# Squares, key scaling and rotary products of layer 1's attention on GpSimd

## The chip, the core and the metric

One core of a Trainium2 chip runs the whole program. Its engines are TensorE (matmul, with its own weight loads), VectorE, ScalarE, GpSimd and SyncE, which issues the transfers. The metric is the device time of one execution in microseconds (us). The kernel before takes 1248.55 us, the median of three runs (1248.15 to 1248.75).

## What is computed

Two decoder layers over 512 tokens of width 1024. Layer 0 mixes tokens with a gated recurrence, layer 1 with multi-head latent attention; beside each mixer four heads attend to a memory of 256 rows, and each layer ends with an MLP that has a causal convolution. The change concerns layer 1's six heads:

```python
q = (rms_norm(cq, qa_g) @ w_uq).reshape(B, S, MLA_HEADS, MLA_QK)              # 128 + 64 columns a head
kv = (rms_norm(ckv, kva_g) @ w_ukv).reshape(B, S, MLA_HEADS, MLA_NOPE + MLA_VDIM)
k_nope, v = kv[..., :MLA_NOPE], kv[..., MLA_NOPE:]
k = jnp.concatenate([k_nope, k_rope], axis=-1)                                # k_rope is the same for all heads
q = rms_norm(q, qn_g)
k = rms_norm(k, kn_g)
q = jnp.concatenate([q[..., :MLA_NOPE], apply_rope(q[..., MLA_NOPE:], cos, sin)], axis=-1)
k = jnp.concatenate([k[..., :MLA_NOPE], apply_rope(k[..., MLA_NOPE:], cos, sin)], axis=-1)
o = causal_block_attention(q, k, v)
```

## The kernel before

All matrix products are made in float32 precision: an operand is split into a rounded high part and the rest (`split`: ScalarE writes the high part, VectorE subtracts), and three matmuls are summed in PSUM. Weights come in tiles of up to 128x1024 (`raw`), are split into `whi` and `wlo`, and stay in a ring of three raw and two split tiles. PSUM has four `acc` tiles for projections, two `at` tiles for scores and two `tp` tiles for transposes.

Layer 1's attention works on three groups g of two heads. The list ORDER names its steps: Q and K project a group's queries and keys (`project_q`, `project_kv`), R normalizes and rotates its queries (`rotary_q`), S scales its keys (`scale_k`), T and U transpose queries and keys of one head, A attends, and M is one half of the memory attention:

```python
ORDER = "Q0 M0 K1 K0 R0 M1 S0 U00 Q1 R1 T00 T01 U01 A00 T10 S1 U10 A01 T11 Q2 K2 U11 S2 A10 A11 R2 U20 U21 T20 T21 A20 A21"
```

This is the order in which the code asks for the steps; the tile scheduler that builds the program then moves instructions, so that steps overlap, and fixes one sequence for each engine at build time. On the chip every engine takes its instructions in that sequence and waits on semaphores where an operand or a buffer isn't ready.

A projection's result leaves PSUM through ScalarE (`ev_q`, `ev_kv`, one for each of four tiles of 128 tokens). There, ScalarE also squares the two heads' columns and sums them (`square_sum`, an activation whose accumulator is read by a second instruction). `rotary_q` and `scale_k` turn the sums into reciprocal roots (`rsqrt`, twelve small VectorE steps), multiply the 64 rotary columns of q by the gain, and rotate them (`rotate`, six VectorE operations of 256 elements). `scale_k` multiplies the keys by the root, one VectorE operation for each tile and head, and writes the scaled rotary key twice into `ks`, as a product and a copy. The scratch of the squares and of the rotation lies in the buffers of the residual's tiles (`head_tile`, xl in the trace). ScalarE then rounds the rotated q (tile `qr`), and VectorE subtracts.

Of the kernel before, what the change touches and what calls it, by code (L numbers as in the profile page):

```python
# [8 lines left out]
F32 = mybir.dt.float32  # L9
# [3 lines left out]
AF = mybir.ActivationFunctionType  # L13
ALU = mybir.AluOpType
AX = mybir.AxisListType

P = 128
# [79 lines left out]
def hybrid_trunk_kernel(ctx, tc, x, mem, params, pos, wts, out, tap):  # L97
# [80 lines left out]
    def tt(o, a, b, op):  # L178
        nc.vector.tensor_tensor(out=o, in0=a, in1=b, op=op)  # L179

# [562 lines left out]
    with ExitStack() as l1:  # L743
# [41 lines left out]
        def rotate(o, a, nh, w):  # L785

            shape = [P, NT, nh, HALF]
            c = cost.unsqueeze(2).broadcast_to(shape)
            s = sint.unsqueeze(2).broadcast_to(shape)
            x1, x2 = a[:, :, :, 0:HALF], a[:, :, :, HALF:]  # L790
            for dst, p, q, op in ((o[:, :, :, 0:HALF], c, s, ALU.subtract), (o[:, :, :, HALF:], s, c, ALU.add)):
                tt(dst, x1, p, ALU.mult)
                tt(w, x2, q, ALU.mult)
                tt(dst, dst, w, op)
# [57 lines left out]
        with tc.tile_pool(name="mla", bufs=1, reuse_waits="tile") as ap:  # L852
# [4 lines left out]
            def project_q(g):  # L857
# [3 lines left out]
                def ev_q(t, ps):  # L861
                    act(q[:, t], ps.rearrange("p (h c) -> p h c", c=QK), AF.Identity, scale=rcq[:, t:t + 1])
                    for h in range(2):
                        square_sum(q[:, t, h, :], QK, qss[:, t, h:h + 1])
# [4 lines left out]
            def square_sum(src, n, o):  # L869
                junk = head_tile(15, (P, QK), F32)  # L870
                act(junk[:, :n], src, AF.Square, accum_out=o)

            def project_kv(g):
# [4 lines left out]
                def ev_kv(t, ps):  # L878
                    act(kv[:, t], ps.rearrange("p (h c) -> p h c", c=2 * P), AF.Identity, scale=rck[:, t:t + 1])
                    for h in range(2):  # L880
                        square_sum(k[:, t, h, :], NOPE, kss[:, t, h:h + 1])
# [4 lines left out]
            def rotary_q(q, qss):  # L886
# [4 lines left out]
                tt(qrope, qrope, pcol("qn").unsqueeze(1).broadcast_to([P, 2 * NT, ROPE]), ALU.mult)  # L891
                rotate(ro, q[:, :, :, NOPE:], 2, head_tile(15, (P, NT, 2, HALF), F32))
# [5 lines left out]
            def scale_k(k, kss):  # L898
# [3 lines left out]
                for t in range(NT):  # L902
                    for h in range(2):
                        ts(k[:, t, h, :], k[:, t, h, :], rk[:, t, h:h + 1], None, ALU.mult)

                ks = ap.tile([P, NT * 2, 2, ROPE], F32, name="ks")
                tt(ks.rearrange("p (t h) a c -> p t h a c", h=2)[:, :, :, 0], kr.unsqueeze(2).broadcast_to([P, NT, 2, ROPE]),
                   rk.unsqueeze(3).broadcast_to([P, NT, 2, ROPE]), ALU.mult)
                nc.vector.tensor_copy(out=ks[:, :, 1], in_=ks[:, :, 0])
# [147 lines left out]
```

## Time and profile before

| what | us |
|---|---|
| median of three runs | 1248.55 |
| the profiled execution | 1248.88 |
| its span on the core | 1246.8 |
| TensorE busy, over the span | 1223.9 (98%) |
| VectorE busy, over the span | 755.1 (61%) |
| ScalarE busy, over the span | 558.5 (45%) |
| GpSimd busy, over the span | 18.7 (2%) |
| layer 1's attention, about | 720 to 850 |

The busy time of an engine is the time in which one of its instructions runs; what an engine waits for is a matter of the sequence, and is read from the waits and the timeline. GpSimd works only at the program's start, where it builds masks.

### The profile page before, as it was taken

Reading aid. Unit: us, or ns where it says so; the run is one execution under the profiler, and the core shown is the slowest. Engines: PE = TensorE matmul, PEld = TensorE weight load, DVE = VectorE, ACT = ScalarE, POOL = GpSimd, SP = SyncE. Lnnn points to the kernel's source line nnn. Section 1 sums busy time; section 2 is a strip of 40 time slices with the busy share of each in tenths; the row PEclk is TensorE's granted clock in tenths of the full one; section 3 lists DMA queues with packets and bytes.
Section 4 is the critical chain, followed back from the end, with each engine's and each line's share of the span. In section 5 each row is a group of like instructions: output and inputs, shape, how many; then the busy total and the mean of one; then the engine's idle time right before and its main releaser. Section 6 shows DMA issues by size and latency. Waiting matters only on the chain.

```text
span 1246.8 us, 15938 instructions
## 1 busy us (share of the span) xinstructions
PE 1223.9 (98%) x6106; PEld 1017.8 (82%) x6106; DVE 755.1 (61%) x1536; ACT 558.5 (45%) x966; POOL 18.7 (2%) x50
## 2 busy tenths in 40 slices
PE   6999999999999999999999999999999999999998
PEld 4869888888888888888889877777888888888887
DVE  6857575765776757652425758765665766764222
ACT  5463434433543434332325689754453444433211
POOL 6000000000000000000000000000000000000000
PEclk9999999999999999999999999999999999999999
DMA  6211222123232233323323312012223233322331
GB/s 238 80 52 60 77 68 69 53 84 91 96 101 101 85 102 101 97 90 101 102 85 111 119 33 77 33 34 68 85 85 102 87 102 99 102 94 92 116 120 51
DMA packets 31755, 110.44 MB, mean 89 GB/s; under 512 B 3776, under 2 KB 4160, under 8 KB 31680
## 3 DMA queue, kind: packets, MB, share of 16 engines
q1 hardware_dynamic: 31680, 109.43, 27.3%
q8 instruction: 48, 0.79, 0.3%
q14 instruction: 27, 0.22, 0.1%
HBM read 107.32 MB, written 2.10 MB: 88 GB/s over the span
## 4 chain that ended last, share of the span: by engine, by line
PE 92%; ACT 4%; DVE 3%; issue 1%; DMA 1%; SPq 0%; DVEq 0%; ACTq 0%
PE acc L171 63%; PE at L171 24%; PE tp L202 3%; PE tp L171 2%; ACT xl L191 1%; DVE wlo L179 1%; ACT whi L191 0%; ACT pr L191 0%; DMA mt<-in_mem 0%; ACT kv L191 0%; ACT yl L191 0%; ACT q L191 0%; ACT xh L191 0%; ACT yh L191 0%; PE at L202 0%
## 5 line engine op out<-in xcount | busy, mean ns | idle before, releaser
L179 DVE TENSOR_TENSOR wlo<-raw,whi 128x1024 fp32r<-128x1024 f32 (+2 forms) x201 | 240.0, 1195 | 374.5 <-ACT whi L191 367.3
L191 ACT ACTIVATE whi<-raw 128x1024 fp32r<-128x1024 f32 (+2 forms) x201 | 208.9, 1039 | 459.2 <-PE acc L171 298.8
L171 PE MATMUL acc<-xh,whi 128*128 128x512 f32 x616 | 241.1, 391 | 0.0
L171 PE MATMUL acc<-xh,wlo 128*128 128x512 f32 x616 | 240.8, 392 | 0.2 <-DVE wlo L179 0.2
L171 PE MATMUL acc<-xl,whi 128*128 128x512 f32 x616 | 240.9, 391 | 0.0
L171 PEld LDWEIGHTS acc<-xh,whi 128*128 128x128 f32 x616 | 115.7, 188 | 24.4 <-issue 1.0
L171 PEld LDWEIGHTS acc<-xh,wlo 128*128 128x128 f32 x616 | 115.5, 188 | 24.0 <-DVE wlo L179 0.4
L171 PEld LDWEIGHTS acc<-xl,whi 128*128 128x128 f32 x616 | 115.7, 188 | 23.6
L182 DVE SCALAR_TENSOR_TENSOR t<-u,par,t 128x510 f32<-128x510 f32 (+1 forms) x176 | 121.6, 746 | 4.2 <-ACT t L191 4.2
L171 PE MATMUL at<-xh,wlo 128*128 128x512 f32 x232 | 90.5, 390 | 0.0
L171 PE MATMUL at<-xl,whi 128*128 128x512 f32 x232 | 90.3, 389 | 0.0
L171 PE MATMUL at<-xh,whi 128*128 128x512 f32 x232 | 90.2, 389 | 0.0
L191 ACT ACTIVATE t<-u,par 128x512 f32<-128x512 f32 x88 | 67.0, 808 | 41.7 <-DVE u L179 41.7
L171 PE MATMUL acc<-wlo,xh 128*128 128x256 f32 (+2 forms) x224 | 67.1, 300 | 1.3 <-DVE wlo L179 1.3
L171 PE MATMUL acc<-whi,xh 128*128 128x256 f32 (+2 forms) x224 | 67.2, 302 | 0.5 <-ACT xh L191 0.4
L171 PE MATMUL acc<-whi,xl 128*128 128x256 f32 (+2 forms) x224 | 67.1, 301 | 0.0
L171 PE MATMUL acc<-whi,ah 128*128 128x512 f32 x132 | 51.3, 389 | 0.0
L171 PE MATMUL acc<-wlo,ah 128*128 128x512 f32 x132 | 51.3, 389 | 0.0
L171 PE MATMUL acc<-whi,al 128*128 128x512 f32 x132 | 51.3, 389 | 0.0
L171 PEld LDWEIGHTS at<-xl,whi 128*128 128x128 f32 x232 | 43.5, 188 | 9.1
L171 PEld LDWEIGHTS at<-xh,wlo 128*128 128x128 f32 x232 | 43.6, 188 | 9.0
L171 PEld LDWEIGHTS at<-xh,whi 128*128 128x128 f32 x232 | 43.5, 188 | 9.0
(333 smaller groups left out, 2143.4 us busy)
## 6 DMA issues: line engine op xcount, KB each, us to landing
raw<-in_w_up SPq DMA_DIRECT2D x88, 512.0 KB, 3.5
raw<-in_w_down SPq DMA_DIRECT2D x44, 512.0 KB, 3.5
raw<-in_hg_w_in SPq DMA_DIRECT2D x26, 512.0 KB, 3.6
raw<-in_w_out SPq DMA_DIRECT2D x16, 512.0 KB, 3.5
raw<-in_w_mem_kv SPq DMA_DIRECT2D x8, 512.0 KB, 4.6
mt<-in_mem SPq DMA_DIRECT2D x4, 512.0 KB, 4.7
xt<-in_x SPq DMA_DIRECT2D x4, 512.0 KB, 8.3
out<-u SPq DMA_DIRECT2D x8, 256.0 KB, 2.0
```

What stands on the lines that cost most here:

```text
L171: nc.tensor.matmul(ps, a, b, start=start, stop=stop)
L179: nc.vector.tensor_tensor(out=o, in0=a, in1=b, op=op)
L182: nc.vector.scalar_tensor_tensor(out=o, in0=a, scalar=s, in1=b, op0=op0, op1=op1)
L191: nc.scalar.activation(out=o, in_=a, func=f, **kw)
L202: nc.tensor.transpose(out=ps, in_=src, identity=ident)
```

## The change

The squares of q and k are made by GpSimd, for both heads of a tile in one product, into a new tile `sq2` with two buffers, and VectorE sums them (`square_sums`); ScalarE's squares are gone. The gain on q's rotary columns and the rotation's six operations are made by GpSimd, through the new helper `ptt`; `rotate` gets the helper as an argument, and the shared rotary key (`krot`) still uses VectorE's. The scaling of the keys is one GpSimd product for each tile of tokens, over both heads, and `ks` is written by two GpSimd products.

```diff
--- before.py
+++ after.py
@@ -177,6 +177,9 @@
 
     def tt(o, a, b, op):
         nc.vector.tensor_tensor(out=o, in0=a, in1=b, op=op)
+
+    def ptt(o, a, b, op):
+        nc.gpsimd.tensor_tensor(out=o, in0=a, in1=b, op=op)
 
     def stt(o, a, s, b, op0, op1):
         nc.vector.scalar_tensor_tensor(out=o, in0=a, scalar=s, in1=b, op0=op0, op1=op1)
@@ -782,7 +785,7 @@
         ssr = zp.tile([P, 32], F32, name="ssr")[:, :NT]
         kr = zp.tile([P, NT, ROPE], F32, name="kr")
 
-        def rotate(o, a, nh, w):
+        def rotate(o, a, nh, w, tt=tt):
 
             shape = [P, NT, nh, HALF]
             c = cost.unsqueeze(2).broadcast_to(shape)
@@ -860,15 +863,15 @@
 
                 def ev_q(t, ps):
                     act(q[:, t], ps.rearrange("p (h c) -> p h c", c=QK), AF.Identity, scale=rcq[:, t:t + 1])
-                    for h in range(2):
-                        square_sum(q[:, t, h, :], QK, qss[:, t, h:h + 1])
+                    square_sums(q[:, t], QK, qss[:, t])
 
                 gemm("mla_w_uq", g, cqh, cql, ev_q, tokens=True)
                 return q, qss
 
-            def square_sum(src, n, o):
-                junk = head_tile(15, (P, QK), F32)
-                act(junk[:, :n], src, AF.Square, accum_out=o)
+            def square_sums(src, n, o):
+                sq = ap.tile([P, 2 * QK], F32, name="sq2", bufs=2)[:, :2 * n].rearrange("p (h c) -> p h c", c=n)
+                ptt(sq, src, src, ALU.mult)
+                nc.vector.tensor_reduce(out=o, in_=sq, op=ALU.add, axis=AX.X)
 
             def project_kv(g):
                 kv = ap.tile([P, NT, 2, NOPE + P], F32, name="kv", bufs=2)
@@ -877,8 +880,7 @@
 
                 def ev_kv(t, ps):
                     act(kv[:, t], ps.rearrange("p (h c) -> p h c", c=2 * P), AF.Identity, scale=rck[:, t:t + 1])
-                    for h in range(2):
-                        square_sum(k[:, t, h, :], NOPE, kss[:, t, h:h + 1])
+                    square_sums(k[:, t], NOPE, kss[:, t])
 
                 gemm("mla_w_ukv", g, ckh, ckl, ev_kv, tokens=True)
                 return k, V, kss
@@ -888,8 +890,8 @@
                 rsqrt(rq.rearrange("p t h -> p (t h)"), qss.rearrange("p t h -> p (t h)"), QK)
                 ro = head_tile(14, (P, NT, 2, ROPE), F32)
                 qrope = q[:, :, :, NOPE:].rearrange("p t h c -> p (t h) c")
-                tt(qrope, qrope, pcol("qn").unsqueeze(1).broadcast_to([P, 2 * NT, ROPE]), ALU.mult)
-                rotate(ro, q[:, :, :, NOPE:], 2, head_tile(15, (P, NT, 2, HALF), F32))
+                ptt(qrope, qrope, pcol("qn").unsqueeze(1).broadcast_to([P, 2 * NT, ROPE]), ALU.mult)
+                rotate(ro, q[:, :, :, NOPE:], 2, head_tile(15, (P, NT, 2, HALF), F32), ptt)
                 qr = ap.tile([P, NT, 2, 2, ROPE], F32R, name="qr")
                 act(qr[:, :, :, 0, :], ro, AF.Copy)
                 tt(qr[:, :, :, 1, :], ro, f32(qr)[:, :, :, 0, :], ALU.subtract)
@@ -900,13 +902,12 @@
                 tt(kss, kss, ssr.unsqueeze(2).broadcast_to([P, NT, 2]), ALU.add)
                 rsqrt(rk.rearrange("p t h -> p (t h)"), kss.rearrange("p t h -> p (t h)"), QK)
                 for t in range(NT):
-                    for h in range(2):
-                        ts(k[:, t, h, :], k[:, t, h, :], rk[:, t, h:h + 1], None, ALU.mult)
+                    ptt(k[:, t], k[:, t], rk[:, t].unsqueeze(2).broadcast_to([P, 2, NOPE]), ALU.mult)
 
                 ks = ap.tile([P, NT * 2, 2, ROPE], F32, name="ks")
-                tt(ks.rearrange("p (t h) a c -> p t h a c", h=2)[:, :, :, 0], kr.unsqueeze(2).broadcast_to([P, NT, 2, ROPE]),
-                   rk.unsqueeze(3).broadcast_to([P, NT, 2, ROPE]), ALU.mult)
-                nc.vector.tensor_copy(out=ks[:, :, 1], in_=ks[:, :, 0])
+                for a in range(2):
+                    ptt(ks.rearrange("p (t h) a c -> p t h a c", h=2)[:, :, :, a], kr.unsqueeze(2).broadcast_to([P, NT, 2, ROPE]),
+                        rk.unsqueeze(3).broadcast_to([P, NT, 2, ROPE]), ALU.mult)
                 return ks
 
             def turned(src):
```

Since the scheduler places every instruction anew, the sequences of TensorE, VectorE and ScalarE differ throughout the attention, from the first query group to the output projection; SyncE's, with all transfers, is the same. Three places follow. Buffers carry a number in their names where there are several; xl are the scratch tiles, yl and yh belong to the memory attention, kv, q and ks to the heads. Line numbers are three higher in the new file from the helper on.

ScalarE before, from the first evacuation of a key and value tile on, behind the first query projection:

```order
L191 ACTIVATE kv<-acc,rck 128x512
L191 ACTIVATE xl_6395,mqss<-q 128x192
L191 ACTIVATE whi<-raw 128x1024
L191 ACTIVATE xl_6397,mqss<-q 128x192
L191 ACTIVATE kv<-acc,rck 128x512
L191 ACTIVATE xl_6403,mqss<-q 128x192
L191 ACTIVATE xl_6405,mqss<-q 128x192
L191 ACTIVATE kv<-acc,rck 128x512
L191 ACT_TABLE_LOAD
```

ScalarE now, from the four evacuations of the same query projection on:

```order
L194 ACTIVATE q<-acc,rcq 128x384 x4
L194 ACTIVATE yh_6430<-tp 128x512
L194 ACTIVATE whi<-raw 128x1024
L194 ACTIVATE kv<-acc,rck 128x512
L194 ACTIVATE qr<-xl_6645 128x8x64
L194 ACTIVATE kv<-acc,rck 128x512
L194 ACT_TABLE_LOAD
L194 ACTIVATE yl_6454,su<-at,nm,rq 128x256
```

Between the evacuations stood the squares; now the copy into qr of group 0 stands ahead of the second evacuation of kv; before, it came only after the third round of exponentials of the memory attention.

GpSimd now, from its first new instruction on (before, its sequence ended with the masks):

```order
L182 TENSOR_TENSOR sq_6379<-q 128x384
L182 TENSOR_TENSOR sq_6386<-q 128x384
L182 TENSOR_TENSOR sq_6393<-q 128x384
L182 TENSOR_TENSOR sq_6400<-q 128x384
L182 TENSOR_TENSOR q<-q,par 128x8x64
L182 TENSOR_TENSOR xl_6645<-q,cost 128x8x32
L182 TENSOR_TENSOR xl_6647<-q,sint 128x256
L182 TENSOR_TENSOR xl_6645<-q,sint 128x8x32
L182 TENSOR_TENSOR xl_6645<-xl_6645,xl_6647 128x8x32
L182 TENSOR_TENSOR sq_6545<-kv 128x256
L182 TENSOR_TENSOR xl_6647<-q,cost 128x256
L182 TENSOR_TENSOR xl_6645<-xl_6645,xl_6647 128x8x32
```

The first four products (sq is the new tile) are the squares of the first query group; then come the gain and the rotation, with the first square of a key tile inside.

VectorE before, at the scaling of group 0's keys, in the second half of the memory attention:

```order
L182 SCALAR_TENSOR_TENSOR mrk<-rs_t,mrk 128x8
L186 TENSOR_SCALAR kv<-kv,mrk 128x128 x8
L179 TENSOR_TENSOR ks<-kr,mrk 128x8x64
L431 RECIPROCAL su<-su 128x4
L909 COPY ks<-ks 128x8x64
L186 TENSOR_SCALAR yl_6740<-yl_6740,su 128x256 x2
L186 TENSOR_SCALAR yl_6741<-yl_6741,su 128x256 x2
```

VectorE now, in the second half of the memory attention:

```order
L434 RECIPROCAL su<-su 128x4
L189 TENSOR_SCALAR yl_6686<-yl_6686,su 128x256 x2
L189 TENSOR_SCALAR yl_6687<-yl_6687,su 128x256 x2
L423 TENSOR_REDUCE nm<-at 128x2
L874 TENSOR_REDUCE mqss<-sq_6854 128x2
L179 TENSOR_TENSOR nm<-nm,rq 128x4
L179 TENSOR_TENSOR wlo<-raw,whi 128x768
L874 TENSOR_REDUCE mqss<-sq_6861 128x2
L434 RECIPROCAL su<-su 128x4
L189 TENSOR_SCALAR yl_6728<-yl_6728,su 128x256 x2
```

The products of the keys have left this place, and sums of squares of the second query group, which GpSimd makes, stand between the softmax steps and the split of a weight tile.

## Rows read from the trace of the kernel before

**Rows 1.** Windows, all engines: stretch, length, busy us (instructions) by engine, clock, DMA.

```profile
720.00:850.00 130.00, 125.15 (x692) 96.78 (x691) 90.71 (x308) 97.96 (x281) 0.00 (x0) 1.00 0.13 42
750.00:780.00 30.00, 28.94 (x172) 23.63 (x170) 25.94 (x96) 27.21 (x81) 0.00 (x0) 1.00 0.26 82
780.00:820.00 40.00, 38.29 (x211) 29.18 (x212) 31.88 (x120) 28.31 (x79) 0.00 (x0) 1.00 0.06 19
```

**Rows 2.** Waits, 720 to 852: who waits for whom, total us, times, longest.

```profile
PEld tp L202 <- ACT xl L191: 2.1, 2, 1.5
```

**Rows 3.** Lines by form, ScalarE, 720 to 852: count, busy us, mean ns, idle before.

```profile
L191 ACT ACTIVATE xl<-q 128x192 f32<-128x192 f32 x24 | 8.9, 372 | 0.2
L191 ACT ACTIVATE xl<-kv 128x128 f32<-128x128 f32 x24 | 8.1, 337 | 0.2
L191 ACT ACTIVATION_READ_ACCUMULATOR xl<-kv 128x1 f32 x24 | 5.4, 224 | 0.0
L191 ACT ACTIVATION_READ_ACCUMULATOR xl<-q 128x1 f32 x24 | 5.0, 206 | 0.0
```

**Rows 4.** The same view, VectorE, 720 to 852.

```profile
L186 DVE TENSOR_SCALAR kv<-kv,mrk 128x128 f32<-128x128 f32 x24 | 5.1, 277 | 0.1
L179 DVE TENSOR_TENSOR ks<-kr,mrk 128x512 f32<-128x512 f32 x3 | 2.0, 683 | 0.0
L909 DVE COPY ks<-ks 128x512 f32<-128x512 f32 x3 | 1.2, 407 | 0.0
L179 DVE TENSOR_TENSOR xl<-q,cost 128x256 f32<-128x256 f32 x6 | 2.5, 419 | 0.0
L942 DVE TENSOR_REDUCE mnm<-at 128x1 f32<-128x384 f32 x6 | 3.3, 548 | 2.8 <-PE at L171 2.8
L942 DVE TENSOR_REDUCE mnm<-at 128x1 f32<-128x256 f32 x6 | 2.5, 417 | 0.2 <-PE at L171 0.2
```

**Rows 5.** Timeline, GpSimd at the end of the masks: start, length, engine, line, operation.

```profile
17.93 0.35 POOL L148 MEMSET mtmp<- 128x128 f32 x2
18.23 0.59 POOL L150 TENSOR_SCALAR_AFFINE_SELECT mtmp<-mtmp 128x128 f32<-128x128 f32 x2
```

**Rows 6.** Timeline, VectorE and GpSimd while the masks are built.

```profile
7.80 0.33 DVE L188 TENSOR_SCALAR rs_v<-mss 128x2 f32<-128x2 f32 x1 [6.02 <-ACT kvf L191]
8.06 1.37 POOL L152 TENSOR_SCALAR_AFFINE_SELECT mask<-mtmp 128x128 int8<-128x128 f32 x2
8.16 0.63 DVE L186 TENSOR_SCALAR rs_t<-rs_v 128x2 int32<-128x2 int32 x1
8.83 0.92 DVE L188 TENSOR_SCALAR rm<-rs_t 128x2 int32<-128x2 int32 x1
9.68 1.03 POOL L150 TENSOR_SCALAR_AFFINE_SELECT mtmp<-mtmp 128x128 f32<-128x128 f32 x2
10.11 0.16 DVE L182 SCALAR_TENSOR_TENSOR rs_t<-rs_t,rs_v 128x2 f32<-128x2 f32 x1
10.48 1.21 DVE L179 TENSOR_TENSOR wlo<-raw,whi 128x1024 fp32r<-128x1024 f32 x1
10.67 2.79 POOL L152 TENSOR_SCALAR_AFFINE_SELECT mask<-mtmp 128x128 int8<-128x128 f32 x2
```

**Rows 7.** Timeline, ScalarE, from the first evacuation of queries on.

```profile
723.40 1.04 ACT L191 ACTIVATE q<-acc,rcq 128x384 f32<-128x384 f32 x2
727.11 0.70 ACT L191 ACTIVATE kv<-acc,rck 128x512 f32<-128x512 f32 x1
729.32 0.70 ACT L191 ACTIVATE kv<-acc,rck 128x512 f32<-128x512 f32 x1
731.43 1.28 ACT L191 ACT_TABLE_LOAD   x1
```

**Rows 8.** Timeline, TensorE, in the key projection and ahead of the memory attention's transposes.

```profile
733.26 0.40 PE L171 MATMUL acc<-whi,ckh 128*128 128x512 f32 x1
741.80 1.15 PE L202 MATMUL tp<-ident,yl 128*128 128x128 f32 x8 [1.12 <-DVE yl L186]
```

## The prediction

> **What bounds the kernel now.** I read the windows first, then the waits, then the lines by form, then the timeline of the places where the edit lands. Layer 1's attention runs from about 720 to 850 us. Over these 130 us TensorE is busy for 125.15 [rows 1], so all that a relief of the other engines can give back here is 4.85 us; VectorE and ScalarE are busy for 91 and 98 us beside it, GpSimd for none. In 750 to 820, where the keys and the second and third query group are prepared and the second memory attention ends, VectorE works 25.94 of 30 and 31.88 of 40 us [rows 1]. TensorE leads, but its transposes need what ScalarE and VectorE hand over in time; the squares on ScalarE are named as what the weight loads of transposes wait for, 2.1 us in all [rows 2]. So the question is not how much work leaves ScalarE and VectorE, but whether GpSimd delivers in time, since each engine takes its instructions in the written order.
>
> **What leaves.** ScalarE loses 24 squares of 192 and 24 of 128 columns with the reading of their sums [rows 3]: 8.9 + 8.1 + 5.4 + 5.0 = 27.4 us. VectorE loses the scaling of the keys (5.1 us), three products for ks with their copies (0.68 + 0.41 each), three gains on q (128x512 too, taken as 0.68) and 18 rotary products and sums of 0.42 [rows 4]: 5.1 + 3.3 + 2.0 + 7.5 = 17.9 us. ScalarE's part is worth at most the 4.85 us that TensorE idles; I take the 2.1 us of [rows 2], **-2.1**.
>
> **What VectorE gets.** 24 sums of squares: 12 over 384 and 12 over 256 elements. The maxima over as many elements take 0.548 and 0.417 us [rows 4], those from PSUM: 6.6 + 5.0 = 11.6 us. Off TensorE's path by themselves; they count below.
>
> **What GpSimd gets.** 63 products and sums of two inputs: 12 of 384, 42 of 256 and 9 of 512 elements. No such row exists before; the nearest are GpSimd's own. A memset of 128 elements takes 0.35 / 2 = 0.175 us and a select with one input 0.59 / 2 = 0.295 [rows 5]: 0.12 us for 128 elements of one input over a fixed 0.175. With two inputs that is 0.655 us for 256, 0.895 for 384, 1.135 for 512, in sum 10.7 + 27.5 + 10.2 = 48.5 us. Lower end: VectorE's prices for the same shapes (0.42, 0.55, 0.68), 30.3 us. Upper end: the whole 0.295 for every 128 elements of each input (1.18, 1.77, 2.36), 92 us. I take 48.5, because it stands on the same engine's rows and grants the fixed part once. (The Trainium skill, GPSIMD Engine Reference, section Performance versus the Vector engine, gives a two-input product of 2048 elements as 1.96 times VectorE's; an estimate from that page would be 59 us, a little over my value, and would make the sum below some 5 us longer. No run here shows it yet.)
>
> **How the two engines disturb each other.** While GpSimd builds its masks at the start of the program, VectorE's small steps stretch: 128x2 operations of 0.16 us take 0.33, 0.63 and 0.92 us beside selects of 0.71 us [rows 6]. The waits are 0.17, 0.47 and 0.76, on average 0.47 or two thirds of one select. The other way round, two selects that take 1.03 us together take 2.79 when VectorE runs its subtraction of 128x1024 from SBUF (1.21 us) [rows 6]. So I charge VectorE two thirds of the length of GpSimd's operations.
>
> **Place A, group 0's rotation in ScalarE's queue: +4.3.** The new order puts the copy into qr right behind the first evacuation of kv; behind it on ScalarE stand the second evacuation, the table load and the first softmax of the memory attention. The first q tile is evacuated at 723.9 [rows 7]. GpSimd then has, before the rotated q is complete, four squares (3.6), the gain (1.1), six rotary steps (3.9) and one square of kv (0.7): 733.2, and one subtraction of 1.2 us in between [rows 6] makes it 734.4. With 0.6 for the copy the second evacuation starts at 735.0 in place of 729.3 and the table load at 735.7 in place of 731.4 [rows 7]. TensorE reaches the second tile of the next projection, which needs that evacuation's PSUM buffer, at 733.26, and it waits today for this very softmax at 741.80 (1.12 us idle, released by VectorE's scaling of its result) [rows 8]. There is no slack, so I take the table load's 4.3 us in full. Bounds: 0 at the lower price (rotation complete at 729.7, as early as ScalarE gets there), 12.7 at the upper (742.8, table load at 744.1).
>
> **Place B, 750 to 820: +9.9.** Here GpSimd gets three times the scaling of keys with ks (4 x 0.655 + 2 x 1.135 = 4.9), two query groups (4 x 0.895 + 1.135 + 6 x 0.655 = 8.65) and two groups of key squares (2.6): 37.2 us. VectorE is busy 57.8 of the 70 us [rows 1], loses 3 x 2.8 for keys and ks, 2 x 3.2 for two rotations and 1.7 for the tail of the first (16.5 in all), gets 8 x 0.417 + 8 x 0.548 = 7.7: 49.0. Two thirds of GpSimd's time on top make 73.8. If the 12.2 us in which VectorE idles today vanish in that, the stretch grows by 3.8 us; if they stay, as waits for TensorE and ScalarE would, by 16.0. Nothing in the rows says which, so I take the middle, +9.9. VectorE's queue holds the softmax steps and the weight splits behind each step that waits, so TensorE follows. Lower bound 0: GpSimd's time wholly beside VectorE's.
>
> **At nothing:** the order on SP doesn't change, so the weights come as before; the code has the same table loads; the new square tiles have two buffers, so a third square waits for VectorE's sum of the first, which is in B.
>
> **Sum.** The profiled execution took 1248.88 us (span 1246.8), 0.3 over the median of the runs. 1248.9 - 2.1 + 4.3 + 9.9 = **1261.0 us**, 1.0% slower.
>
> **Rivals.**
> 1. *The two engines don't disturb each other, and GpSimd is as quick as VectorE.* Then the relief remains: all 4.85 us of TensorE's idle time, 1244.0 us. For it: ScalarE and VectorE are at 75 and 70% in this stage. Against it: [rows 6]. Chance 0.11.
> 2. *GpSimd at the lower price, disturbing as measured.* A is 0; in B 37.2 shrinks to 23.2, two thirds are 15.5, VectorE needs 64.5 of 70, and the middle of 0 and 6.7 is 3.3: 1248.9 - 2.1 + 3.3 = 1250.1, no change that can be told. Chance 0.11.
> 3. *VectorE stands still for the whole of each GpSimd operation.* B is 49.0 + 37.2 - 70 = 16.2 with no idle left: 1248.9 - 2.1 + 4.3 + 16.2 = 1267.3, slower. It decides from the point where VectorE's queue is never empty when a GpSimd operation starts; the 0.92 us step is the row for it, the 0.33 us step the row against. (The Trainium skill, SBUF — State Buffer, section Who interferes with whom, calls the port pair of the two engines an exclusive lock, held for a whole instruction. The 0.92 us agrees, the mean of the three rows is two thirds.) Chance 0.18.
> 4. *GpSimd itself is the bound, at the upper price.* A is 12.7; in B 37.2 grows to 70.8, two thirds are 47.2, and 49.0 + 47.2 - 70 = 26.3: 1248.9 - 2.1 + 12.7 + 26.3 = 1285.8. The one-input select is against it, as a memset already takes 0.175 of its 0.295. Chance 0.10.
>
> **How the numbers follow.** The forecast has 0.50. Less than 0.2% (2.5 us) can't be told from no change. Faster is rival 1, 0.11; the same is rival 2, 0.11; slower is the rest, 0.78. The range from 1246 to 1284 leaves out rival 1 and most of rival 4, about 0.19, and holds the spread of B (3.8 to 16.0) and most of A's.
>
> **What would show it.** In the changed profile: GpSimd's 128x256 product near 0.65 us; ScalarE idle for some 6 us ahead of the first copy into qr, near 728 to 734; VectorE's 128x8 and 128x256 steps longer by up to a GpSimd operation between 750 and 820; TensorE's idle time in the attention at 15 us or more. It would be wrong if that copy starts before 730, if VectorE's small steps keep their 0.16 us beside GpSimd, or if GpSimd's products take over 1 us for 256 elements.

## The result, and the profile after

The changed kernel takes 1267.54 us (median of four runs, 1267.01 to 1267.92) beside 1248.65 for the kernel before (1248.15 to 1249.07): 1.5% slower, ratio 1.0151 with a 95% interval of 1.0134 to 1.0167. The prediction said 1261.0 us, 1246 to 1284, and slower with a chance of 0.78. The direction and the range hold; the time is 6.5 us off, and its terms are off by more, in both directions, so that the small error of the total is in part luck.

The first line of the page of after gives busy time, share of the span and instructions of each engine.

```profile
PE 1233.1 (97%) x6106; PEld 1023.4 (81%) x6106; DVE 762.9 (60%) x1509; ACT 543.4 (43%) x870; POOL 69.0 (5%) x113
```

The span is 1265.6 us, 18.8 more than before. TensorE runs the same 6106 matmuls and is busy for 9.2 us longer (1233.1 for 1223.9), and it is idle for 9.6 us more (1265.6 - 1233.1 = 32.5 for 22.9). So half of the loss is waiting, and half is matmuls that take longer. The windows say where; the columns are those of [rows 1], and the third from the end is the granted TensorE clock, as a share of 2.4 GHz.

```profile
730.00:740.00 10.00, 5.71 (x24) 4.44 (x22) 4.60 (x19) 5.57 (x13) 5.03 (x9) 0.82 0.12 39
740.00:750.00 10.00, 10.00 (x38) 8.10 (x39) 7.02 (x19) 6.81 (x16) 3.04 (x5) 0.67 0.08 22
750.00:820.00 70.00, 64.57 (x356) 48.47 (x354) 53.21 (x159) 43.12 (x98) 32.52 (x42) 0.98 0.13 46
720.00:850.00 130.00, 116.37 (x597) 89.32 (x596) 87.83 (x247) 72.55 (x157) 49.67 (x63) 0.92 0.13 42
720.00:870.00 150.00, 135.51 (x696) 103.24 (x695) 98.77 (x282) 83.72 (x185) 49.67 (x63) 0.93 0.11 37
```

Where [rows 1] have 125.15 us of TensorE and a clock of 1.00 in 720 to 850, after has 116.37 and 0.92. Place A of the prediction stands in 730 to 740. These are ScalarE's instructions there, to be read beside [rows 7], and TensorE's beside [rows 8] (start, length, engine, line, operation, and in brackets the idle time and what ended it):

```profile
726.61 0.69 ACT L194 ACTIVATE kv<-acc,rck 128x512 f32<-128x512 f32 x1 [0.20 <-PE acc L171]
734.40 0.63 ACT L194 ACTIVATE qr<-xl 128x512 fp32r<-128x512 f32 x1 [7.11 <-POOL xl L182]
734.94 0.67 ACT L194 ACTIVATE kv<-acc,rck 128x512 f32<-128x512 f32 x1
735.62 1.28 ACT L194 ACT_TABLE_LOAD   x1
```

```profile
733.50 0.39 PE L171 MATMUL acc<-wlo,ckh 128*128 128x512 f32 x1
738.17 0.58 PE L171 MATMUL at<-kth,yh 64*128 64x256 f32 x1 [4.29 <-ACT yl L194]
```

The copy into qr waits 7.11 us for the rotation, and the second evacuation of keys, the table load and the softmax wait behind it. The rotation was forecast complete at 734.4 and the table load at 735.7; the copy behind the rotation starts at 734.40 and the table load at 735.62. TensorE pauses for 4.29 us. What was not forecast is the next thing: during that pause the granted clock falls from 1.00 to 0.50, from 2.4 to 1.2 GHz, and it stays there for 10.2 us. It falls twice more. Windows over the three stretches:

```profile
736.40:746.60 10.20, 8.43 (x28) 6.86 (x29) 7.20 (x25) 7.56 (x20) 1.80 (x3) 0.50 0.07 21
770.50:773.90 3.40, 3.40 (x12) 1.80 (x12) 3.40 (x9) 1.19 (x2) 3.32 (x5) 0.50 0.15 51
821.70:828.50 6.80, 5.88 (x18) 4.37 (x19) 2.83 (x9) 1.64 (x4) 1.18 (x2) 0.50 0.01 2
```

TensorE is busy for 17.7 us in these three stretches; half of that, 8.9 us, is nearly all of the 9.2 us that it is busy longer. The starts of successive matmuls of 512 columns lie 0.42 us apart in the first stretch and 0.23 right behind it. The kernel before has no such stretch.

```profile
745.20 0.63 PE L171 MATMUL acc<-whi,ckh 128*128 128x512 f32 x1
745.62 0.63 PE L171 MATMUL acc<-wlo,ckh 128*128 128x512 f32 x1
...
746.77 0.39 PE L171 MATMUL acc<-wlo,ckh 128*128 128x512 f32 x1
747.00 0.39 PE L171 MATMUL acc<-whi,ckl 128*128 128x512 f32 x1
```

GpSimd's products by form, 715 to 850 (count, busy us, mean ns, idle before):

```profile
L182 POOL TENSOR_TENSOR sq<-q 128x384 f32<-128x384 f32 x12 | 10.5, 891 | 722.9 <-ACT q L194 721.1 <-DVE pr L189 1.8
...
L182 POOL TENSOR_TENSOR sq<-kv 128x256 f32<-128x256 f32 x12 | 7.4, 628 | 13.3 <-ACT kv L194 9.9 <-DVE nm L179 2.3 <-DVE mkss L874 1.1
L182 POOL TENSOR_TENSOR ks<-kr,mrk 128x512 f32<-128x512 f32 x6 | 6.2, 1060 | 0.1
...
L182 POOL TENSOR_TENSOR xl<-xl,xl 128x256 f32<-128x256 f32 x6 | 4.4, 728 | 0.2
```

Two more mechanisms show in the timelines. One is VectorE's queue: TensorE waits for the split of the memory attention's queries, which on VectorE stands behind sums that wait for GpSimd's squares (VectorE, then TensorE's next matmul):

```profile
726.64 0.55 DVE L874 TENSOR_REDUCE mqss<-sq 128x2 f32<-128x384 f32 x1 [0.23 <-POOL sq L182]
727.11 0.68 DVE L179 TENSOR_TENSOR yh<-tp,yh 128x512 fp32r<-128x512 f32 x1
...
727.84 0.39 PE L171 MATMUL at<-kth,yh 64*128 64x256 f32 x2 [1.05 <-DVE yh L179]
```

The other shows at the third group's keys. VectorE's steps, GpSimd's products and TensorE's transposes between 818 and 823:

```profile
818.61 0.47 DVE L179 TENSOR_TENSOR rs_t<-mrq 128x8 f32<-128x8 f32 x1
819.11 0.54 DVE L185 SCALAR_TENSOR_TENSOR rs_t<-rs_t,rs_v 128x8 f32<-128x8 f32 x1
819.68 0.54 DVE L185 SCALAR_TENSOR_TENSOR mrq<-rs_t,mrq 128x8 f32<-128x8 f32 x1
...
820.71 1.27 DVE L189 TENSOR_SCALAR pr<-pr,msu 128x384 f32<-128x384 f32 x1
```

```profile
818.44 2.33 POOL L182 TENSOR_TENSOR kv<-kv,mrk 128x256 f32<-128x256 f32 x4 [7.27 <-DVE rs_t L185]
820.73 2.15 POOL L182 TENSOR_TENSOR ks<-kr,mrk 128x512 f32<-128x512 f32 x2
```

```profile
822.03 0.90 PE L205 MATMUL tp<-ident,pr 128*128 128x128 f32 x3 [2.49 <-DVE pr L189]
```

The same steps in the kernel before, among VectorE's forms, 720 to 852:

```profile
L182 DVE SCALAR_TENSOR_TENSOR rs_t<-rs_t,rs_v 128x8 f32<-128x8 f32 x18 | 2.8, 159 | 0.2
...
L186 DVE TENSOR_SCALAR pr<-pr,msu 128x384 f32<-128x384 f32 x6 | 2.5, 419 | 0.2
```

Steps of 128x8 that take 0.16 us there take 0.47 to 0.54, and the scaling of 384 columns takes 1.27 where it has 0.42. Each of them ends 0.02 to 0.22 us behind the end of a product of GpSimd, as if it had waited for it; the experiment shadow tests that. TensorE waits 2.49 us for that scaling, and the last stretch at half clock begins in this wait.

### The profile page after: what moved, and what is told of

The parts are those of the page before. It is cut to its first block, busy times and chain, and to the rows that moved or that the text cites. A ratio compares the mean times of both kernels' runs of the same rounds, so it can differ in the third digit from the quotient of the medians.

```text
span 1265.6 us, 15922 instructions
## 1 busy us (share of the span) xinstructions
PE 1233.1 (97%) x6106; PEld 1023.4 (81%) x6106; DVE 762.9 (60%) x1509; ACT 543.4 (43%) x870; POOL 69.0 (5%) x113
## 4 chain that ended last, share of the span: by engine, by line
issue 56%; PE 37%; DVE 4%; POOL 1%; ACT 1%; DMA 1%; SPq 0%; POOLq 0%; DVEq 0%; ACTq 0%
PE acc L171 24%; PE at L171 10%; PE tp L205 2%; PE tp L171 1%; POOL xl L182 1%; POOL sq L182 1%; DMA mt<-in_mem 0%; DVE wlo L179 0%; DVE mnm L943 0%; DVE pr L189 0%; ACT yl L194 0%; ACT pr L194 0%; DVE yl L189 0%; DVE rs_t L185 0%; DVE rs_t L179 0%
## 5 line engine op out<-in xcount | busy, mean ns | idle before, releaser
L179 DVE TENSOR_TENSOR wlo<-raw,whi 128x1024 fp32r<-128x1024 f32 (+2 forms) x201 | 241.7, 1203 | 373.4 <-ACT whi L194 366.3
L171 PEld LDWEIGHTS acc<-xl,whi 128*128 128x128 f32 x616 | 115.7, 188 | 23.6
```

The lines of the kernel that those rows point to most:

```text
L171: nc.tensor.matmul(ps, a, b, start=start, stop=stop)
```

## The experiments

All times are medians; ratios are to the kernel before on the same chip in the same comparison (1248.65 to 1249.05 us). Busy and idle are TensorE's over the span, from the pages.

| kernel | us | ratio's 95% interval | TensorE busy | idle |
|---|---|---|---|---|
| before | 1248.65 | | 1223.9 | 22.9 |
| after | 1267.54 | 1.0134 to 1.0167 | 1233.1 | 32.5 |
| shadow | 1269.22 | 1.0154 to 1.0184 | 1231.6 | 35.6 |
| shadow_memset | 1252.74 | 1.0018 to 1.0045 | 1228.6 | 23.6 |
| shadow_small | 1264.96 | 1.0113 to 1.0147 | 1231.7 | 31.3 |
| sq_only | 1253.65 | 1.0024 to 1.0054 | 1224.9 | 26.5 |
| rot_only | 1256.18 | 1.0043 to 1.0073 | 1226.1 | 28.4 |
| key_only | 1255.68 | 1.0041 to 1.0071 | 1225.6 | 28.0 |
| qr_vector | 1263.02 | 1.0098 to 1.0128 | 1230.1 | 30.8 |
| tt_form | 1265.31 | 1.0116 to 1.0150 | 1232.8 | 31.2 |
| all_vector | 1254.16 | 1.0031 to 1.0061 | 1226.0 | 26.1 |
| pause_only | 1249.76 | 1.0001 to 1.0019 | 1223.3 | 23.6 |
| no_squares | 1249.31 | 0.9999 to 1.0018 | 1223.9 | 22.8 |
| nothing_moved | 1249.66 | 0.9995 to 1.0013 | 1226.1 | 23.0 |

### shadow: GpSimd's work without its results

```diff
+            def idle_work(first, sizes):
+                d = ap.tile([P, 512], F32, name="dum", bufs=1)
+                ptt(d[:, 511:512], first, first, ALU.mult)
+                for n in sizes:
+                    ptt(d[:, :n], par[:, :n], par[:, 8:8 + n], ALU.mult)
 ...
+                idle_work(rk[:, 0, 0:1], 4 * [256] + 2 * [512])
```

> The kernel before, with GpSimd given the 63 products of the change (24 for the squares, 21 for the rotations, 18 for the keys and ks; same sizes) as work that nobody reads: constants into a scratch, each batch started by a one-column read of the q, kv, mrk or mrq that releases it in the change. All other engines keep the sequence of before. This prices the disturbance alone, without GpSimd's latency in any chain. Theory 1 (VectorE's steps stand still behind GpSimd's instructions, and TensorE follows): VectorE's small steps and its scalings stretch by 0.3 to 0.8 us each; 1252 to 1257 us, no pause of TensorE over 2 us. Rival (only the longer way through GpSimd costs, the disturbance disappears in VectorE's idle time): 1247.5 to 1250 us, with the same stretched steps off the path. A third one (they don't disturb each other): VectorE's steps keep their length, 1248.6.

1269.22 us, as slow as the changed kernel, though nothing waits for a result of GpSimd and all other engines run the sequence of before. VectorE's forms, 720 to 870:

```profile
L189 DVE TENSOR_SCALAR kv<-kv,mrk 128x128 f32<-128x128 f32 x24 | 12.3, 574 | 0.1
...
L179 DVE TENSOR_TENSOR mnm<-mnm,mrq 128x1 f32<-128x1 f32 x24 | 6.1, 252 | 0.2
...
L179 DVE TENSOR_TENSOR xl<-tp,xl 128x512 fp32r<-128x512 f32 x6 | 4.1, 689 | 1.6 <-ACT xl L194 1.5
L955 DVE TENSOR_REDUCE mnm<-at 128x1 f32<-128x512 f32 x6 | 4.1, 686 | 1.1 <-PE at L171 1.1
```

GpSimd's idle product, same view:

```profile
L182 POOL TENSOR_TENSOR dum<-par 128x256 f32<-128x256 f32 x42 | 35.7, 851 | 3.3
```

The scaling of keys takes 574 ns where [rows 4] have 277, the product of one column 252 for the 152 of the kernel before; the maximum over PSUM keeps its 0.68, and so does the subtraction whose one operand lies in PSUM. Sorted by whether a GpSimd product is running when the VectorE step before has ended, the scalings of keys take 0.32 us in the mean without one and 0.87 with one, and the 128x8 steps 0.16 and up to 0.70; the 22 maxima, reciprocals and subtractions with an operand in PSUM that meet one keep their length. Where VectorE has the turn, it is GpSimd's product that takes longer: 0.85 us in the mean for 256 columns, 0.72 at the shortest.

In all VectorE is busy 23.9 us longer by the page (779.0 for 755.1) beside 68.4 us more of GpSimd (87.1 for 18.7). That is more of GpSimd than the change brings (49.67 us, in the window of 720 to 870 above): 30 products of one column start the batches, the idle products take 0.72 us at the shortest where the changed kernel's squares of 256 columns take 0.61, and VectorE still has the work that the change takes from it. So the disturbance alone can cost as much as the change does; that it is the whole loss of the changed kernel isn't shown by it.

Theory 1 has the mechanism, but its time is too low: it expected no pause of TensorE over 2 us, and there are three of 2.0 to 3.6. The two rivals, that the disturbance hides in VectorE's idle time or isn't there, fall. The Trainium skill, SBUF — State Buffer, section Who interferes with whom, says that a VectorE instruction with two operands from SBUF contends with a GpSimd instruction that reads SBUF, that tensor_scalar and copy can contend with GpSimd, and that reductions on trn2 never do. The trace agrees in all three.

The clock in the same run:

```profile
720.00:762.00 42.00, 39.17 (x211) 30.36 (x209) 31.33 (x84) 36.98 (x118) 26.03 (x38) 1.00 0.15 50
765.90:772.70 6.80, 5.31 (x17) 3.01 (x19) 4.38 (x11) 2.45 (x8) 2.70 (x5) 0.50 0.21 77
793.30:800.10 6.80, 5.57 (x14) 3.78 (x15) 6.80 (x12) 0.60 (x1) 6.41 (x9) 0.50 0.01 2
```

For 42 us both engines disturb each other and the clock is full; it falls in the pauses of TensorE that begin at 763.1 (3.63 us) and at 791.7 (2.87 us), and a third time at 834.2, for 3.4 us, behind one of 2.00 us.

### shadow_memset and shadow_small: what GpSimd does, and in what pieces

Both edits are against shadow.

```diff
-                    ptt(d[:, :n], par[:, :n], par[:, 8:8 + n], ALU.mult)
+                    for _ in range(2):
+                        nc.gpsimd.memset(d[:, :n], 0.0)
```

> As shadow (the kernel before with idle work on GpSimd, all other engines in the sequence of before), but each of the 63 products is two memsets of the same columns, which read nothing. At the program's start a memset of 128 columns takes 0.2 us, so the 126 make some 30 to 45 us of GpSimd time. Theory 1 (what stands in VectorE's way is the read of two operands from SBUF by GpSimd, which takes turns with VectorE's own two-operand reads and scalings; sums, maxima and steps with a PSUM operand kept their length in shadow): VectorE's steps keep their length beside memsets, 1248.5 to 1250.5 us. Rival (any instruction of GpSimd holds VectorE up): steps stretch by the length of a memset, 1255 to 1265.

1252.74 us: 3.8 us lost in place of 20, with 46.7 us of memsets. VectorE's forms, 720 to 870:

```profile
L189 DVE TENSOR_SCALAR kv<-kv,mrk 128x128 f32<-128x128 f32 x24 | 7.4, 481 | 0.1
...
L179 DVE TENSOR_TENSOR mnm<-mnm,mrq 128x1 f32<-128x1 f32 x24 | 3.6, 151 | 0.2
...
L185 DVE SCALAR_TENSOR_TENSOR rs_t<-rs_t,rs_v 128x8 f32<-128x8 f32 x18 | 2.8, 161 | 0.2
...
L923 DVE COPY ks<-ks 128x512 f32<-128x512 f32 x3 | 1.5, 490 | 0.0
```

Products of two operands keep their 151 ns beside memsets, and the rsqrt steps theirs; scalings and copies stretch still (481 ns for 277, 490 for 407). For 54.4 us more of GpSimd (73.1 for 18.7) VectorE is busy 3.8 us longer (758.9 for 755.1), where shadow has 23.9 for 68.4. So it is mostly the reading of operands, as theory 1 has it, but not only: the tensor_scalar and the copy are held up by memsets too, the time is above theory 1's range, and the rival has a part.

```diff
-                    ptt(d[:, :n], par[:, :n], par[:, 8:8 + n], ALU.mult)
+                    for c in range(0, n, 128):
+                        ptt(d[:, c:c + 128], par[:, c:c + 128], par[:, c + 8:c + 136], ALU.mult)
```

> As shadow, but every idle product is cut in pieces of 128 columns: 2, 3 or 4 for one, 156 in all, the same elements. By the fixed part of an instruction (0.61 for 256 and 0.83 for 384 columns alone: 0.22 us for 128 more, 0.17 fixed) GpSimd has 156 x 0.39 = 61 us in place of 48. Theory 1 (the engines take turns instruction by instruction, so a VectorE step waits for one piece at most): a step's stretch falls from 0.3-0.7 to under 0.4 us; 1256 to 1264 us, less than shadow's 1269.2. Rival (VectorE loses GpSimd's whole time, however it is cut): 1269 plus two thirds of the 13 us more, 1275 to 1282.

1264.96 us, between shadow_memset and shadow. Its scaling of keys among VectorE's forms, 720 to 870, takes 402 ns where shadow's takes 574:

```profile
L189 DVE TENSOR_SCALAR kv<-kv,mrk 128x128 f32<-128x128 f32 x24 | 8.2, 402 | 0.1
```

GpSimd is busy 19.4 us longer than in shadow (106.5 for 87.1), and yet the kernel is 4.3 us faster. That fits engines that take turns instruction by instruction, so that a step loses the rest of the piece that is running. The rival (the whole of GpSimd's time counts) falls; theory 1's range, 1256 to 1264, is missed by 1.

### sq_only, rot_only, key_only: one part at a time

Each is the change without the other two parts: of `ptt` there remain the squares with VectorE's sums; or the gain and the rotation; or the scaling of the keys with ks.

> Only the squares of the change (GpSimd multiplies, VectorE sums); gain, rotation, keys and ks on VectorE as before. The copy into qr then stands behind the first softmax of the memory attention in ScalarE's queue, so place A is gone. Theory 1 (disturbance by the amount of GpSimd work, plus place A): GpSimd has 18 of 50 us, VectorE 11.6 us more; 1250 to 1255 us. Rival (every us of GpSimd costs the same, wherever it stands): 18 / 50 of the 18.9 us, 1255.4. Second rival (the relief of ScalarE shows): 1244 to 1247.

> Only the gain and the rotation of the change on GpSimd (21 products, some 18 us); squares on ScalarE, keys and ks on VectorE as before. The copy into qr stands far behind the first softmax in ScalarE's queue, three exponentials into the second half of the memory attention, so group 0 has time. Theory 1 (what costs is the copy into qr ahead of the softmax, which is not there, and some disturbance): 1248 to 1253, no TensorE pause over 2 us, full clock throughout. Rival (the longer rotation costs wherever it stands): 18 / 50 of 18.9, 1255.4.

> Only the scaling of the keys and ks on GpSimd (18 products, 14 us); squares on ScalarE and the rotation on VectorE as before. With the squares alone the kernel was 4.7 us slower than before, with the rotation alone 7.2. Theory 1 (each part costs by what it holds up where it stands; place A, 4.4 us of pause and 5.1 of half clock, belongs to none of the parts alone but to squares and rotation together): keys alone 1249 to 1253 us, at full clock. Rival (the parts add up, no interplay): 18.9 - 4.7 - 7.2 = 7.0, so 1256.

1253.65, 1256.18 and 1255.68 us: 4.7, 7.2 and 6.7 us slower, together 18.6, as much as the whole change (each over the kernel before in its own comparison, 1248.94 or 1248.99). For squares and rotation theory 1's ranges take in the first and miss the second by 3; for keys it said 1249 to 1253, and the rival, that parts add up, said 1256. The rotation's rival, a share by the amount of GpSimd's work, said 1255.4 and is nearer than theory 1 too. So my account by places doesn't explain the sum. What the pages show is that the mixture differs: the three alone have 3.6 + 5.5 + 5.1 = 14.2 us more idle and 1.0 + 2.2 + 1.7 = 4.9 more busy time, the whole has 9.6 and 9.2. Whether the equal total is more than chance is open; rot_only's profiled execution also has 3.4 us at half clock near 663, ahead of the attention, which the change didn't bring. Each part alone has the pauses of its own steps: sq_only 1.05 us at 726.5 (VectorE's sums, as above) with a full clock to the end, rot_only 2.16 us at 812.4 and key_only 2.54 us at 820.2, both times transposes of pr behind stretched VectorE steps. Two more don't fit theory 1: rot_only pauses 1.96 us at 760.4 for a weight split that its own order puts behind the scaling of keys, and key_only, for which it expected a full clock, has 3.4 us at half clock at 762.9, behind pauses of 1.25 and 0.61 us.

### qr_vector: ScalarE freed from place A

```diff
-                act(qr[:, :, :, 0, :], ro, AF.Copy)
+                nc.vector.tensor_copy(out=qr[:, :, :, 0, :], in_=ro)
```

> The changed kernel with one edit: the copy into qr is VectorE's, so that no evacuation and no softmax of ScalarE stands behind the rotation (on VectorE it takes the place just ahead of the subtraction, which waits for the rotation in any case). Theory 1 (place A: a pause of 4.4 us, and the 10.2 us at half the clock behind it come from that pause): the pause near 733 shrinks to under 2 us and no half clock follows there; 1267.5 less 4.4 and 5.1 is 1258, with 2 us of later give and take 1256 to 1261. Rival (the half clock has another cause than the pause): the pause goes and the half clock stays, 1263. Second rival (VectorE, standing at the copy, is late for the second softmax, and the pause only moves): 1265 to 1268.

1263.02 us: 4.5 us below the changed kernel. ScalarE, then VectorE:

```profile
731.16 1.28 ACT L194 ACT_TABLE_LOAD   x1
734.12 0.56 ACT L194 ACTIVATE yl<-at,nm,rq 128x256 f32<-128x256 f32 x1 [1.68 <-DVE nm L179]
```

```profile
733.41 0.42 DVE L874 TENSOR_REDUCE mkss<-sq 128x2 f32<-128x256 f32 x1 [2.09 <-POOL sq L182]
733.75 0.34 DVE L179 TENSOR_TENSOR nm<-nm,rq 128x4 f32<-128x4 f32 x1
```

The table load is back at 731.16, but the softmax starts at 734.12 all the same, because its maxima are multiplied on VectorE behind a sum that waits 2.09 us for a square, which GpSimd makes among the rotation's steps. So 1.68 us of place A stood in VectorE's queue, hidden behind the part in ScalarE's. The pause of 4.29 us is replaced by two, of 1.00 us at 734.4 and 1.17 us at 739.3 (the one of 1.05 us at 727 stands in both kernels), and the clock falls for 6.8 us in place of 10.2. My expectation (no half clock with pauses under 2 us, and 1256 to 1261 us) is wrong; the rival that gave 1263 has the time but not the reason, since the stretch did shrink.

### tt_form: another form of the scalings

```diff
-                    ts(pr[:, :n], pr[:, :n], su, None, ALU.mult)
+                    tt(pr[:, :n], pr[:, :n], su.broadcast_to([P, n]), ALU.mult)
```

(and the same for yl)

> The changed kernel with one edit: the scalings of the softmax rows (pr in the attention, yl in the memory attention) are tensor_tensor with the reciprocal broadcast along the row, where the change has tensor_scalar. In the profile of after the scalings of 128x256 take 0.68 us in the mean beside GpSimd and 0.35 in before, and the 128x8 tensor_scalars up to 0.72, while sums, maxima and tensor_tensors keep their length. Theory 1 (GpSimd holds up VectorE only in that form): the scalings take a tensor_tensor's 0.42 us for 256 columns beside GpSimd too, the pauses of TensorE at the transposes of yl near 767 to 770 go, 1262 to 1266 us. Rival (it holds up every form that reads SBUF): 0.42 plus 0.3 to 0.8 us, 1268 to 1272. Place A stands in both, with its 4.4 us pause and its stretch at the half clock.

1265.31 us, but not for theory 1's reason. The scalings of the memory attention among VectorE's forms, 720 to 870:

```profile
L179 DVE TENSOR_TENSOR yl<-yl,su 128x256 f32<-128x256 f32 x16 | 9.5, 652 | 0.3
```

The scaling takes 652 ns in the mean where the form has 0.42 alone, and up to 1.31. A step that reads two operands from SBUF is held up as a tensor_scalar is; the expectation's reading that tensor_tensors keep their length in the changed kernel was wrong, as its 128x8 steps of L179 above show. The 2.2 us below the changed kernel are at the edge of what can be told, since the two intervals overlap, and the scheduler chose another sequence for TensorE, VectorE and ScalarE with the new form; whether one of its moves earned them is open.

### all_vector: the same work on VectorE

```diff
-        nc.gpsimd.tensor_tensor(out=o, in0=a, in1=b, op=op)
+        nc.vector.tensor_tensor(out=o, in0=a, in1=b, op=op)
```

> The changed kernel with its 63 products on VectorE in place of GpSimd, which does nothing in the attention. VectorE gets 24 squares (11.6 us by the prices of the same shapes) and 24 sums (11.6) on top of before: 114 of the 130 us. ScalarE stays relieved of its squares. Theory 1 (it is GpSimd, by taking turns with VectorE and by its longer chains, that costs): no stretched steps, VectorE fuller; 1250 to 1257 us, 10 or more below the changed kernel. Rival (moving the squares off ScalarE costs, whoever makes them, since VectorE's queue is what TensorE waits for): 1262 to 1268.

1254.16 us: 13.4 us less than the changed kernel and 5.2 more than before. So, by the totals, some 13 of the 19 us belong to GpSimd, by turns and by its longer chains, which this run doesn't part, and some 5 to what the move of the squares and their sums costs VectorE's queue. This is no exact split: the sequences differ, and VectorE makes the squares here, which it doesn't in the changed kernel. The one large pause is that of a weight split behind squares and sums. TensorE's timeline, and the windows of the pause and of what follows:

```profile
761.09 0.45 PE L171 MATMUL acc<-wlo,cqh 128*128 128x384 f32 x1 [3.68 <-DVE wlo L179]
```

```profile
757.20:761.10 3.90, 0.22 (x3) 0.01 (x1) 3.90 (x11) 2.98 (x10) 0.00 (x0) 1.00 0.00 0
761.40:764.80 3.40, 3.29 (x15) 2.29 (x14) 3.40 (x16) 1.20 (x2) 0.00 (x0) 0.50 0.45 154
```

GpSimd does nothing here, no step is stretched, and the clock falls as well, for 3.4 us behind the pause. Together with shadow's first 42 us, in which GpSimd works and the clock is full, this parts the clock from GpSimd's work: it goes with TensorE's pauses.

### pause_only: a pause alone

```diff
+                for _ in range(24):
+                    nc.gpsimd.memset(d[:, :510], 0.0)
+                act(d[:, 510:511], d[:, 0:1], AF.Copy)
```

> The kernel before with one wait: 24 memsets of 510 columns run on GpSimd from the first q tile on, and ScalarE copies one column of their result just ahead of the table load of the memory attention's first softmax. No other engine's sequence changes, GpSimd reads nothing and does nothing else. By the memsets of shadow_memset (0.545 us for 512 columns) they end at 724.2 + 13.1 = 737.3, so the table load comes 5 to 6 us later than at 731.43, and TensorE pauses for about 6 us near 734, with no work added to it. Theory 1 (a pause of TensorE brings the clock down to its half level for a while, and that is what the second half of the loss is): a stretch at half clock of 7 to 14 us behind the pause; 1249 + 5.5 + 4 is 1258.5, so 1257 to 1261. Rival (the lower clock in the changed kernel comes with GpSimd's and VectorE's work, not with the pause): full clock, 1253 to 1255.5.

1249.76 us, and it tells little: 11 of the 24 memsets, which don't touch the column that the read writes, ran at 702 us, ahead of it, so ScalarE waited for the rest only for a short time, as its timeline shows:

```profile
731.54 0.20 ACT L191 ACTIVATE dum<-dum 128x1 f32<-128x1 f32 x1 [0.86 <-POOL dum L861]
```

TensorE paused for 0.69 us behind it, and the clock stayed full. So the test of a long pause without other work was not made; all_vector's pause, with GpSimd at rest, is the nearest to it.

### no_squares and nothing_moved: what could be gained

```diff
-                act(junk[:, :n], src, AF.Square, accum_out=o)
+                act(o, src[:, 0:1], AF.Square)
```

> The kernel before without the squares of q and k: in place of a square and sum over 192 or 128 columns ScalarE squares the first column of each head, so the norms are not those of the reference; nothing goes to another engine. This prices the relief of ScalarE alone, 27.4 us less about 5 for the 48 short instructions. Theory 1 (the term of the prediction, 2.1 us, which is what the weight loads of transposes waited for squares): 1246 to 1247.5 us. Rival (all of TensorE's 4.85 us of idle time goes): 1244. Second rival (the relief is worth nothing, since ScalarE's queue isn't what ends last): 1248 to 1249.5.

1249.31 us, no gain: the interval of the ratio is 0.9999 to 1.0018. The waits of the weight loads, 720 to 850, to be read beside [rows 2]:

```profile
PEld tp L202 <- ACT kv L191: 1.5, 1, 1.5
...
PEld tp L202 <- ACT q L191: 1.4, 1, 1.4
```

Without the squares the same weight loads wait for what stood behind the squares, the evacuations themselves.

```diff
+                ro = q[:, :, :, NOPE:]
 ...
-                        ts(k[:, t, h, :], k[:, t, h, :], rk[:, t, h:h + 1], None, ALU.mult)
```

> The kernel before without any of the work that the change moves: squares reduced to one column for each head (as in no_squares), no gain and no rotation (the copy into qr reads q), no scaling of the keys, ks written once for all groups. So queries and keys are not those of the reference, and no engine gets anything in exchange. This bounds what any placement of that work could gain. Theory 1 (TensorE bounds this stage, and its remaining 4.85 us of idle time come from other chains: leaving out the squares alone gave 1249.3 against 1248.9): 1246 to 1249 us. Rival (VectorE's rotary and key work is what TensorE's idle time comes from, so it goes): 1243.5 to 1245.5.

1249.66 us, 0.9995 to 1.0013. VectorE and ScalarE have 12 and 11 us less to do in 720 to 850 than in [rows 1], and TensorE is as busy as there:

```profile
720.00:850.00 130.00, 124.40 (x692) 97.27 (x691) 78.79 (x260) 87.03 (x234) 0.00 (x0) 1.00 0.13 42
```

So this work costs the kernel before nothing that can be measured where it is, and a placement that only takes it off ScalarE and VectorE has nothing to gain. The scheduler set another sequence for the rest in both of these runs, so what a better sequence could gain isn't shown. For the squares the second rival (worth nothing) holds; for all of the work the time is just above theory 1's range, and the rival falls.

## Why the prediction came out as it did

**The relief, -2.1: wrong.** No run shows it: 1249.31 and 1249.66 us without the work, for 1248.94 and 1249.05 with it. The step that failed is reading the 2.1 us of [rows 2] as what ends when the named releaser goes; the next releaser came as late.

**GpSimd's prices: right.** For 256, 384 and 512 columns 0.655, 0.895 and 1.135 us were taken; alone, 256 columns take 0.61 (after at 732.26), 384 take 0.83 (785.09), 512 take 1.09 and less; the rotation's pieces of 32 columns take 0.73. GpSimd is busy 49.67 us for the 63 products, 48.5 were forecast. The Trainium skill's GPSIMD Engine Reference, section Performance versus the Vector engine, has 1.96 times VectorE for 2048 columns; here it is 0.61 to 0.42 for 256 columns, 1.45 times, and the estimate of 59 us from it was too high.

**How the engines disturb each other: the mechanism right, the size wrong.** Two thirds of GpSimd's time were charged to VectorE. In after VectorE is busy 762.9 us where 755.1 - 17.9 + 11.6 = 748.8 would be undisturbed: 14.1 us by this estimate, 0.28 of GpSimd's 49.67; in shadow 0.35. A step waits only if it is of a locking kind and meets a running product, and VectorE's reductions and PSUM steps, a large part of its time here, never wait. Rival 3 (VectorE stands still for the whole) has the measured time, 1267.3, by luck, since its mechanism is refuted by these shares.

**Place A, +4.3: right to the tenth** on ScalarE (734.40, 735.62, a pause of 4.29), and incomplete: VectorE's part of it (qr_vector) and the clock behind it were not seen. It was also charged whole, though the wait of 1.12 us at 741.80 that [rows 8] show in the kernel before doesn't occur in the changed one.

**Place B, +9.9: too large.** All idle time grew by 9.6 us; without place A's 4.3 some 5.3 are left, and they include the 1.05 us at 726.8 that the prediction had at nothing, because it looked at the buffers of the squares and not at what stands behind the sums in VectorE's queue. In 750 to 820, which holds less of the work now that the kernel is late, VectorE is idle for 16.8 us (70 - 53.21) where it was for 12.2; so the idle time didn't vanish, and the picture of a VectorE that is filled up by GpSimd's turns is not what happened. What cost TensorE time there were mostly single waits behind VectorE's stretched steps.

**The clock: missing, +9.2.** A pause of TensorE was priced at its length. The 16 stretches at half clock in the attentions of after and of the experiments, 3.4 to 10.2 us each, all begin within an idle time of TensorE or at most 1.7 us behind one, from several pauses of 0.2 to 0.6 us (shadow_memset, 762 to 766) up to one of 4.3; the other way round it isn't so, as sq_only's two pauses of 1.05 and 1.04 us leave the clock full. What length of pause it takes, the runs don't tell.

The sum by its terms is then 0 + 4.3 + 5.3 + 9.2 = 18.8, where -2.1 + 4.3 + 9.9 = 12.1 was forecast. The missing clock (9.2) and the relief that wasn't there (2.1) left the forecast 11.3 too low, and a place B that was 4.6 too dear took part of that back, so the total is only 6.7 short; that it stayed in the range is in part luck. Of what was to show it: the price of a product, ScalarE idle for 7.11 us ahead of the copy, and stretched 128x8 steps are there; TensorE's idle time in the attention is 14.5 us (150 - 135.51, the window of 720 to 870 above), just under the 15 that were named.

## What to carry to other kernels

Before work is taken off an engine, leave it out in a trial: if the time stays, as here, taking it off that engine has nothing to gain, however busy the engine looks. GpSimd beside VectorE costs VectorE the rest of a running product for every step that reads two operands from SBUF, scales or copies there, so give it such work only where VectorE's steps reduce or read PSUM, and in short pieces (1264.96 us with pieces of 128 columns, 1269.22 without). And where TensorE bounds a stage, a pause of some microseconds can cost about twice its length, because the matmuls behind it may run at half the clock for a while: place A's 4.29 us brought 8.43 us of matmuls at half clock, some 4.2 more.

## What the runs showed of the hardware

- The granted clock fell to 0.50 for 10.2 us in the middle of a program, from within a pause of 4.3 us on. The Trainium skill, TensorE: Matmul & The Clock Gate, Part 1, tells of the two levels and that TensorE's own activity sets them; the runs agree. It isn't the same in every execution: a pause of 1.34 us near 661 us, ahead of the attention, stands in all 14 traces, and in three of them (rot_only, shadow_memset, nothing_moved) 3.4 us at half clock follow it. By an estimate, half of those 3.4 us, a single execution can be 1.7 us longer for that alone.
- A memset on GpSimd, which reads nothing, holds up VectorE's tensor_scalar (0.48 us in the mean for 128 columns, 0.28 without) and copies (0.49 for 0.41), but not its products of two SBUF operands (0.15 us with and without).
- A VectorE step with an operand in PSUM doesn't wait for GpSimd's turns: 128x512 subtractions with one keep 0.68 to 0.69 us beside running products.
